# A gated decoder block on one core: the attention branch as seven half-size products, with pooling sums and operand sums on GpSimd

## The chip, the cores and the metric

The kernel runs on one core of a Trainium2 chip. Five engines work beside each other, each with its own queue of instructions: TensorE (PE in the profile, its weight loads PEld), VectorE (DVE), ScalarE (ACT), GpSimd (POOL) and SyncE (SP, which here only issues DMA transfers). The metric is the device time of one execution in microseconds, the median of several.

## The reference

A decoder block on 1024 tokens of 1024 channels, float32. Two mixers run in parallel, a pooling over windows of 2, 4, 8 and 16 tokens and a sliding-window attention; each goes through a branch matrix, is multiplied by its gate, and the sum goes through W_out. An MLP follows.

```python
POOL_WINDOWS = (2, 4, 8, 16)
...
def _multiscale_pool(u, w_pool, pool_scale):
...
        pooled.append((upper - lower) / count)
    pooled = jnp.stack(pooled, axis=2)
    diff = (pooled - uf.reshape(B, S, N_POOL_GROUPS, POOL_GC)).astype(u.dtype)
    mixed = jnp.einsum('bsgc,gcd->bsgd', diff, w_pool)
...
        g = jax.nn.sigmoid(gates.astype(jnp.float32)).astype(x.dtype)
        g_pool, g_attn = g[..., :D_MODEL], g[..., D_MODEL:]
        merged = (g_pool * jnp.einsum('bsc,cd->bsd', y_pool, w_branch_pool[l])
                  + g_attn * jnp.einsum('bsc,cd->bsd', y_attn, w_branch_attn[l]))
        mix = jnp.einsum('bsd,de->bse', merged, w_out[l])
        x = x + _rmsnorm(mix, g_mix_post[l])
```

The attention branch, the part that the change is about, multiplies y_attn (1024 tokens by 512 channels) with w_branch_attn (512 by 1024).

## The kernel before

Activations are kept feature-major: channels on the 128 partitions, the 1024 tokens as two halves of 512 columns. Every float32 operand is split into two parts, a high one that a cast makes (L101, mostly ScalarE) and a low one that a subtraction makes (L104, VectorE), so a product takes three matmul passes: high by high, high by low, low by high.

The stages that matter here follow each other on TensorE: the gates' first products (to about 211 us), the rest of the gates (to 320.5), the attention branch (to 364.0), the pooling branch (to 407.5), W_out, the MLP.

**The gates** (class `Pairs`, L444) are computed as a two-by-two block product with seven half-size products in place of eight. A pair of output rows needs seven weight operands; `operand` (L461) makes sums of weight blocks on VectorE (L467, L470, L474, L477) and splits them (L104). Products 1 and 2 are made in an earlier pass. `rest` (L508) makes 6, 7, 5, 4 and 3 for a pair, twelve matmuls each, and closes each with an addition on VectorE that reads the product out of PSUM (L515, L522, L526, L529, L535), five a pair. Then each gate row is multiplied by the tokens' norm factors (`gate_close1` at L700 over 1024 columns, `gate_close0` at L696 over 512), goes through the sigmoid on ScalarE (L692), and is stored to DRAM by a transfer that ScalarE issues (L693). Eight pairs run through this; a pair is 60 matmuls.

**The attention branch** (`branch`, L908) is a plain product: for each of eight output rows `load_w` (L416) loads and splits a weight tile, and `mm_fm` (L423) makes 24 matmuls, into one PSUM bank for each half of the tokens (L428 and L430). VectorE multiplies the result with the gate (L916). The activations are loaded and split by `load_attn` (L876), called from the last gate pair.

**The pooling sums** (`pool_in`, L668) run on VectorE beside the attention branch: a group's window sum is made by doublings (additions over the whole row, L675, with a short copy for the first columns, L676), then scaled and subtracted (L679 to L681). `pool_part` (L918) loads a group, calls it and splits the result (yphi, yplo) for the pooling branch.

**W_out's operands** are sums of blocks; SP loads one block and GpSimd adds the other by a DMA that accumulates (`wo_add`, L948); a one-column copy by GpSimd (L943) holds the load back until a gate tile is done.

**What sets the order.** In the gates' first pass PE, VectorE, ScalarE and SP stand in an order written out by hand. From `rest` on, a scheduler orders the instructions of each engine, and tile pools decide when a buffer is free. GpSimd serves attention in the early stage, up to 172 us, and then stands idle until 351 us.

Of the kernel before, what the change touches and what calls it, by code (L numbers as in the profile page):

```python
# [14 lines left out]
P = 128  # L15
# [35 lines left out]
def block_kernel(ctx: ExitStack, tc, xt, x, consts, vecs, sinks, b_qkv, g_post, g_mlp_post,  # L51
# [35 lines left out]
    def bank(tag, shape=None):  # L87
        return psum["pool"].tile([P] + (shape or [512]), F32, tag=tag, name=nm(tag), bufs=psum["bufs"][tag])
# [4 lines left out]
    def flat(t):  # L93
        return t.rearrange("p a b -> p (a b)")
# [4 lines left out]
    def split(hi, lo, src, eng=dve, first=None):  # L99
        if first is None:  # L100
            act.copy(hi, src)  # L101
        else:
            first.tensor_copy(hi, src)
        eng.tensor_tensor(lo, src, f32(hi), ALU.subtract)  # L104
# [339 lines left out]
    class Pairs:  # L444


        def __init__(self, src, big, result, close_first, close0, close1):
            self.src, self.big, self.result = src, big, result
            self.close_first, self.close0, self.close1 = close_first, close0, close1
            self.X = {n: [None] * 4 for n in OPERAND.values()}  # L450
            self.raw, self.w, self.sums, self.f0, self.b1 = {}, {}, {}, {}, {}
# [38 lines left out]
        def mm(self, b, p, i, kts=range(4), after=False):  # L490
            w, xo = self.w[p, i], self.X[OPERAND[i]]
            for kt in kts:
                for j, (wh, xh) in enumerate(PASSES):
                    pe.matmul(b, w[:, wh, kt, :], xo[kt][:, xh, :], start=not after and kt == 0 and j == 0,  # L494
                              stop=kt == 3 and j == 2, skip_group_check=after)
# [9 lines left out]
            self.mm(b, p, 2, after=True)  # L505
            self.close_first(self.f0[p][:, :512], b)

        def rest(self, p, f1, b6, b7, b5, done=(), then=None, b4=None):  # L508


            f0 = self.f0.pop(p)
            u2 = f0[:, 512:]
            if 6 not in done:
                self.mm(b6, p, 6)
            dve.tensor_tensor(u2, u2, b6, ALU.add)  # L515
            if p in self.b1:
# [6 lines left out]
            if then:  # L523
                then()
            self.mm(b5, p, 5)
            dve.tensor_tensor(f1[:, 512:], v7, b5, ALU.add)  # L526
            if b4 is None:
                self.mm(b7, p, 4, after=True)
                dve.tensor_tensor(f1[:, :512], u2, b7, ALU.add)  # L529
            else:  # L530
                self.mm(b4, p, 4)
                dve.tensor_tensor(v7, v7, b4, ALU.add)
            self.close1(2 * p + 1, f1)
            self.mm(b5, p, 3, after=True)
            dve.tensor_tensor(u2, u2, b5, ALU.add)  # L535
            self.close0(2 * p, f0)

# [12 lines left out]
    def ar(shape):  # L550
        return ga_.tile([P] + shape, F32R, tag="ga", name=nm("ar"))
# [113 lines left out]
                return  # L665
            owed[0] -= c

    def pool_in(gi, u, place):  # L668

        w = WINDOWS[gi]  # L670
# [9 lines left out]
        dve.tensor_tensor(src[:, :w - 1], src[:, :w - 1], cst[:, C_CNT:C_CNT + w - 1], ALU.mult)  # L680
        dve.tensor_tensor(u[:, :w - 1], src[:, :w - 1], u[:, :w - 1], ALU.subtract)  # L681
        yield

    def y_place():
        return flat(yy.tile([P, 2, 512], F32, tag="y", name=nm("t")))


    def gate_first(f, b):
        dve.tensor_tensor(f, b, rb[:, :512], ALU.mult)
# [13 lines left out]
    def gate_result():  # L703
        return flat(yy.tile([P, 2, 512], F32, tag="y", name=nm("z")))
# [115 lines left out]
    def g32(shape):  # L820
        return gp.tile([P] + shape, F32, tag="g", name=nm("g"))
# [9 lines left out]
    def first(p):  # L831
        gt.m1(p, bank("mm"), g32([S]) if 2 <= p < NHELD else None)
# [10 lines left out]
    with tc.manual_schedule(engines={mybir.EngineType.PE, mybir.EngineType.DVE, mybir.EngineType.Activation,  # L843
# [7 lines left out]
        for p in range(NG0):  # L851
# [19 lines left out]
            elif p == 6:  # L871
                gt.load(2)
                gt.load(3, g32([NK, P]))
    asp = [[None, None], [None, None]]

    def load_attn():  # L876
        for kh in range(2):
            for th in range(2):
                ws = stage([2, 512])
                nc.sync.dma_start(ws, y_dram[th][:, 2 * kh:2 * kh + 2])  # L880
                hi = xp.tile([P, 2, 512], F32R, tag="x", name=nm("yahi"))
                lo = xp.tile([P, 2, 512], F32R, tag="x", name=nm("yalo"))
                split(hi, lo, ws)
                asp[th][kh] = (hi, lo)

    for p in range(8):
        if NHELD <= p + 1 < 8:
            gt.f0[p + 1] = gate_result()
            nc.sync.dma_start(gt.f0[p + 1], z_dram[2 * p + 2])
        if p > 1:  # L890
            gt.load(2 * p)
            gt.load(2 * p + 1, g32([NK, P]) if p > 2 else None)
        for i in (6, 7, 5, 4, 3) if p else (5, 4, 3):
            gt.operand(p, i)
        tag = "at" if p % 2 == 0 else "mm"
        gt.rest(p, gate_result(), bank(tag), bank(tag), bank(tag), then=load_attn if p == 7 else None,
                b4=None if p else bank("mm"))


    zg = {}  # L900

    def gate_pair(base, j):
        zg[base, j] = [g32([2, 512]) for _ in range(2)]
# [4 lines left out]
    def branch(w, rhs, base, m):  # L908
        if m % 2 == 0:
            gate_pair(base, m // 2)  # L910
        z = zg[base, m // 2]
        whi, wlo = load_w(w, [4, P])
        bs = [bank("mm"), bank("mm")]
        mm_fm(bs, whi, wlo, rhs, 4)
        for th in range(2):
            dve.tensor_tensor(z[th][:, m % 2], z[th][:, m % 2], bs[th], ALU.mult)  # L916

    def pool_part(gi):  # L918
        u = yy.tile([P, S], F32, tag="y", name=nm("d"))
        nc.sync.dma_start(u, u_dram[gi])  # L920
        for _ in pool_in(gi, u, y_place):
            pass
        hi = xp.tile([P, S], F32R, tag="x", name=nm("yphi"))
        lo = xp.tile([P, S], F32R, tag="x", name=nm("yplo"))
        split(hi, lo, u)
        ysp[gi] = hi, lo

    gop, wop = {}, {}

    def split_pairs(srcs, place, behind=None):  # L930
        ops = [(place([2, 512]), place([2, 512])) for _ in srcs]
        for hi, _ in ops if behind else ():
            pool.tensor_copy(hi[:, 0, :1], behind[:, 0, :1])
        for (hi, lo), t in zip(ops, srcs):
            split(hi, lo, t)
        return ops

    W_Q = {(a, b): w_o[4 * b:4 * b + 4, :, 512 * a:512 * a + 512] for a in range(2) for b in range(2)}

    def wo_load(quad, place, behind=None):  # L940
        ts = [place([2, 512]) for _ in range(2)]
        for t in ts if behind else ():
            pool.tensor_copy(t[:, 0, :1], behind[:, 0, :1])  # L943
# [11 lines left out]
    def bc32(shape):  # L955
        return bcp.tile([P] + shape, F32, tag="bc", name=nm("s3"))

    ysp = {}
    for m in range(8):
        branch(w_ba[m], lambda k, hl, th: asp[th][k // 2][hl][:, k % 2, :], 8, m)  # L960
        if m == 4:
            sums = wo_load((1, 0), a32, zg[8, 2][1])
            wo_add(sums, (1, 1))
        if m in (2, 3, 5, 6):
            pool_part({2: 1, 3: 0, 5: 2, 6: 3}[m])

    def merge(j):
        for z, zp in zip(zg[8, j], zg.pop((0, j))):
# [1 line left out]

    def merged(kh, th):
        return [zg[8, 2 * kh + j][th] for j in range(2)]

    def x_place(shape):
        return xp.tile([P] + shape, F32R, tag="x", name=nm("wo"))

    b11, b12 = merged(0, 1), merged(0, 0)
    for m in range(8):
# [567 lines left out]
```

## Time and profile before

| | |
|---|---|
| time, median of 3 runs | 1110.98 us (1109.47 to 1111.28) |
| the profiled execution's own time | 1111.93 us |
| its span, first to last instruction | 1110.2 us |
| mean granted TensorE clock | 0.999 |
| ScalarE busy | 549.3 us (49%), 917 instructions |
| DMA | 203.18 MB, mean 183 GB/s |

The page gives busy times by engine, then the chain of work that ended last. A row of the timeline is start, duration, engine, line, operation, output<-input and tile size, all in us; in brackets the idle time before it and what released it. A row of a group ends with its count, busy us and mean ns, and the idle time before. A row of the stretches is a window of the span, with busy us and count of each engine, the granted clock, the DMA share and GB/s.

### The profile page before, as it was taken

The numbers are of one execution on the slowest core, as the hardware profiler recorded it, in microseconds if no ns is written. First come the engines' busy times: TensorE is split into PE (matmuls) and PEld (weight loads), VectorE is DVE, ScalarE is ACT, GpSimd is POOL, SyncE is SP. The second block draws the span as 40 slices with busy tenths as digits, with TensorE's granted clock in tenths as the row PEclk, the third lists the DMA queues.
The fourth block names the chain that finished last, engine by engine and source line by source line (L and its number), as shares of the span: only waits on it lengthen the run. The fifth ranks groups of instructions, "written<-read, shape, count | busy, mean of one in ns | idle before, by whom it ended". The sixth has DMA issues, their size and how long they took to land.

```text
span 1110.2 us, 13876 instructions
## 1 busy us (share of the span) xinstructions
PE 1099.0 (99%) x5119; PEld 908.9 (82%) x5119; DVE 806.3 (73%) x1174; ACT 549.3 (49%) x917; POOL 61.3 (6%) x107
## 2 busy tenths in 40 slices
PE   9999999999999999999999999999999999999997
PEld 7888788888888888878888888888888888888885
DVE  5578867899768796889888767666548944456596
ACT  7466656444432337577555655444434434344342
POOL 0334220000001120000000000000000000000000
PEclk9999999999999999999999999999999999999999
DMA  9405578365677581571457655435596635534672
GB/s 349 140 11 135 150 150 292 122 204 209 212 254 258 150 188 58 193 262 38 151 202 257 237 178 195 155 143 207 172 376 216 204 97 174 178 102 153 201 239 108
DMA packets 88419, 203.18 MB, mean 183 GB/s; under 512 B 7328, under 2 KB 19744, under 8 KB 88352
## 3 DMA queue, kind: packets, MB, share of 16 engines
q1 hardware_dynamic: 76208, 176.35, 47.4%
q10 hardware_dynamic: 5616, 19.66, 4.6%
q0 software_dynamic: 6528, 6.29, 4.1%
q8 instruction: 40, 0.66, 0.2%
q14 instruction: 27, 0.22, 0.1%
HBM read 146.70 MB, written 55.57 MB: 182 GB/s over the span
## 4 chain that ended last, share of the span: by engine, by line
PE 87%; DVE 6%; ACT 2%; DMA 2%; issue 1%; SPq 0%; DVEq 0%; ACTq 0%
PE mm L494 24%; PE at L494 16%; PE at L1390 16%; PE mm L1390 12%; PE mm L428 5%; PE mm L187 3%; PE mm L430 3%; PE mm L584 2%; PE at L196 1%; PE at L1032 1%; PE mm L1032 1%; PE sc L187 1%; PE at L399 1%; PE sc L335 1%; PE mm L196 1%
## 5 line engine op out<-in xcount | busy, mean ns | idle before, releaser
L1390 PE MATMUL at<-ar,wh 128*128 128x512 f32 x744 | 169.6, 389 | 0.0
L1390 PEld LDWEIGHTS at<-ar,wh 128*128 128x128 f32 x744 | 139.6, 188 | 29.3 <-DVE ar L104 0.4
L104 DVE TENSOR_TENSOR wh<-raw,wh 128x1024 fp32r<-128x1024 f32 x53 | 64.8, 1223 | 100.5 <-ACT wh L101 100.4
L1390 PE MATMUL mm<-ar,wh 128*128 128x512 f32 x576 | 131.0, 389 | 0.0
L101 ACT CAST wh<-raw 128x1024 fp32r<-128x1024 f32 x53 | 55.7, 1051 | 147.9 <-PE at L1390 72.1
L1390 PEld LDWEIGHTS mm<-ar,wh 128*128 128x128 f32 x576 | 108.1, 188 | 22.4
L101 ACT CAST wh<-st 128x512 fp32r<-128x512 f32 (+1 forms) x97 | 61.6, 645 | 76.1 <-PE at L494 19.1
L104 DVE TENSOR_TENSOR wh<-st,wh 128x512 fp32r<-128x512 f32 (+1 forms) x97 | 68.8, 719 | 29.4 <-ACT wh L101 27.1
L494 PE MATMUL mm<-gr,wh 128*128 128x512 f32 x333 | 80.4, 391 | 0.6 <-DVE gr L1071 0.6
L494 PEld LDWEIGHTS mm<-gr,wh 128*128 128x128 f32 x333 | 62.1, 188 | 13.7 <-DVE gr L1071 1.0
L494 PE MATMUL mm<-T,wx 128*128 128x512 f32 x288 | 67.6, 389 | 0.0
L494 PEld LDWEIGHTS mm<-T,wx 128*128 128x128 f32 x288 | 54.1, 188 | 11.2
L494 PE MATMUL at<-T,wx 128*128 128x512 f32 x252 | 59.1, 389 | 0.0
L494 PEld LDWEIGHTS at<-T,wx 128*128 128x128 f32 x252 | 47.3, 188 | 9.8
L494 PE MATMUL mm<-x,wh 128*128 128x512 f32 x240 | 55.2, 389 | 0.0
L494 PEld LDWEIGHTS mm<-x,wh 128*128 128x128 f32 x240 | 45.0, 188 | 9.4
L584 PE MATMUL mm<-x,wh 128*128 128x512 f32 x192 | 47.8, 396 | 0.0
L104 DVE TENSOR_TENSOR ar<-B,ar 128x1024 fp32r<-128x1024 f32 x37 | 45.1, 1219 | 3.1 <-ACT ar L101 3.0
L584 PEld LDWEIGHTS mm<-x,wh 128*128 128x128 f32 x192 | 35.2, 188 | 7.7
L101 ACT CAST ar<-B 128x1024 fp32r<-128x1024 f32 x37 | 38.8, 1049 | 4.9 <-DVE B L1365 2.8
L494 PE MATMUL at<-gr,wh 128*128 128x512 f32 x150 | 36.6, 390 | 0.0
L101 ACT CAST wx<-ws 128x512 fp32r<-128x512 f32 x30 | 18.6, 619 | 33.1 <-DVE ws L470 18.2
(387 smaller groups left out, 2162.6 us busy)
## 6 DMA issues: line engine op xcount, KB each, us to landing
raw<-f_dram SPq DMA_DIRECT2D x53, 512.0 KB, 3.7
f_dram<-g SPq DMA_DIRECT2D x30, 512.0 KB, 3.3
B<-in_w_dn_dram SPq DMA_DIRECT2D x24, 512.0 KB, 6.5
st<-in_w_up_dram SPq DMA_DIRECT2D x20, 512.0 KB, 3.8
st<-in_w_g_dram SPq DMA_DIRECT2D x18, 512.0 KB, 4.4
f_dram<-g ACTq DMA_DIRECT2D x17, 512.0 KB, 2.7
g<-spill_dram SPq DMA_DIRECT2D x16, 512.0 KB, 5.6
raw<-in_w_dn_dram SPq DMA_DIRECT2D x16, 512.0 KB, 4.5
```

What stands on the lines that cost most here:

```text
L101: act.copy(hi, src)
L104: eng.tensor_tensor(lo, src, f32(hi), ALU.subtract)
L187: pe.matmul(bq, xs_[k][n // 4][:, xh, n % 4 * P:(n % 4 + 1) * P], wq[k][:, h, :], start=k == 0 and j == 0, stop=k == NK - 1 and j == 2)
L196: pe.matmul(bkv_of(n), xs_[k][n // 4][:, xh, n % 4 * P:(n % 4 + 1) * P], wkv[k // 2][:, h, k % 2, :], start=k == 0 and j == 0 and not (joi ...
L335: pe.matmul(sb[:, kv, i, :nk], qt[r, qx, m * P:(m + 1) * P], kx[r, k0:k0 + nk], start=j == 0, stop=j == 2)
L399: pe.matmul(flat(yb), v[:, kv, :], flat(p[:, 4 * kv:4 * kv + 4]), start=j == 0, stop=j == len(mms) - 1)
L428: pe.matmul(bs[th], whi[:, k, :], rhs(k, hl, th), start=k == 0 and hl == 0, stop=False)
L430: pe.matmul(bs[th], wlo[:, k, :], rhs(k, 0, th), start=False, stop=k == nk - 1)
L494: pe.matmul(b, w[:, wh, kt, :], xo[kt][:, xh, :], start=not after and kt == 0 and j == 0, stop=kt == 3 and j == 2, skip_group_check=after)
L584: pe.matmul(b, (whi, wlo)[h][:, k, :], xr(k, xh, th), start=j == 0, stop=j == len(mms) - 1)
L1032: pe.matmul(bs[t], gop[i][kt // 2][gh][:, kt % 2, t * P:(t + 1) * P], wop[i][kt // 2][wh][:, kt % 2], start=not after and kt == 0 and j == ...
L1390: pe.matmul(bs[t], fo[fh][:, k2, t * P:(t + 1) * P], wo_[wh][:, k2, :], start=not after and s2 == 0 and k2 == 0 and j == 0, stop=s2 == NS ...
```

## The change

Five things change, all between the gates' first pass and W_out.

1. The attention branch becomes a class `Halves`: a two-by-two block product by seven half-size products. Four operands of the activations are taken as they are (B11, B21, B22 and, for T1 to T4, sums made by GpSimd in place by `sums`); three sums of weight blocks a pair are made by GpSimd in `weights` and split there (768 columns), the four plain blocks by VectorE. A pair's products go into two PSUM banks: 1, 2, 6, 7 and 4 add up in one, 5 and 3 in the other; after each step that is needed alone the bank is read out and the next product adds to it.
2. The pooling sums go from VectorE beside the branch to GpSimd beside the gates: `diff_sums` for groups 3, 2, 1 and 0 (windows of 16, 8, 4 and 2), called from pairs 0 to 3, which adds, scales by a table and subtracts, and stores the result back to DRAM by GpSimd's queue. `pool_load` and `pool_split` then only load and split it.
3. `Pairs.rest` calls `side()` after each of its steps, by which the operands of the next pair, the splits of B11 to T3 and GpSimd's work are placed between the products; product 3 is issued ahead of close1.
4. SP and GpSimd stand in program order from the gates' second half to the end of the branch.
5. `wo_load` and `wo_add` for the block (1,0) of W_out stand with pairs 2 and 3 of the branch, without the one-column copies.

```diff
-        def rest(self, p, f1, b6, b7, b5, done=(), then=None, b4=None):
+        def rest(self, p, f1, b6, b7, b5, done=(), side=lambda: None, b4=None):
...
+            side()
+            self.mm(b5, p, 3, after=True)
             self.close1(2 * p + 1, f1)
-            self.mm(b5, p, 3, after=True)
...
+    def diff_sums(gi, place):
+
+        w, u = WINDOWS[gi], diffs.pop(gi)
         act.activation(u, u, AF.Identity, bias=vec[:, V_BU + gi:V_BU + gi + 1])
         src, step = u, 1
         while step < w:
             t = place()
-            dve.tensor_tensor(t[:, step:], src[:, step:], src[:, :S - step], ALU.add)
-            dve.tensor_copy(t[:, :step], src[:, :step])
+            pool.tensor_tensor(t[:, step:], src[:, step:], src[:, :S - step], ALU.add)
+            pool.tensor_copy(t[:, :step], src[:, :step])
             src, step = t, 2 * step
-            yield
-        dve.scalar_tensor_tensor(u[:, w - 1:], src[:, w - 1:], 1.0 / w, u[:, w - 1:], ALU.mult, ALU.subtract)
...
+        cn = cst[:, C_CNT:C_CNT + w]
+        pool.tensor_tensor(src[:, w - 1:], src[:, w - 1:], cn[:, w - 1:].broadcast_to([P, S - w + 1]), ALU.mult)
+        pool.tensor_tensor(src[:, :w - 1], src[:, :w - 1], cn[:, :w - 1], ALU.mult)
+        pool.tensor_tensor(u, src, u, ALU.subtract)
+        pool.dma_start(u_dram[gi], u)
...
+        PRODUCT = {1: ("A11", "B11"), 2: ("A12", "B21"), 3: ("S4", "B22"), 4: ("A22", "T4"),
+                   5: ("S1", "T1"), 6: ("S2", "T2"), 7: ("S3", "T3")}
...
+        def sums(self, part):
+            b11, b12, b21, b22 = (self.raw[q] for q in ((0, 0), (0, 1), (1, 0), (1, 1)))
+            if part == 0:
+                pool.tensor_tensor(b11, b12, b11, ALU.subtract)
+                pool.tensor_tensor(b12, b22, b12, ALU.subtract)
+            else:
+                pool.tensor_tensor(b22, b22, b11, ALU.subtract)
+                pool.tensor_tensor(b21, b21, b22, ALU.subtract)
...
+            pool.tensor_tensor(t[:, 0], a21, a22, ALU.add)
+            pool.tensor_tensor(a21, a11, a21, ALU.subtract)
+            pool.tensor_tensor(t[:, 1], t[:, 0], a11, ALU.subtract)
+            pool.tensor_tensor(t[:, 2], a12, t[:, 1], ALU.subtract)
...
+                split(rh, rl, r.rearrange("p m (h k) n -> p (m h) k n", h=2))
+                split(sh, sl, t[:, :3], pool)
...
+        def mm(self, b, p, i, after=False):
+            wn, xn = self.PRODUCT[i]
+            w, xo = self.wops[p][wn], self.ops[xn]
+            for kt in range(2):
+                for j, (wh, xh) in enumerate(PASSES):
+                    pe.matmul(b, w[wh][:, kt, :], xo[xh][:, kt, :], start=not after and kt == 0 and j == 0,
+                              stop=kt == 1 and j == 2, skip_group_check=after)
...
+            self.mm(y, p, 5)
+            act.copy(t2[:, 0], y)
+            sides[0]()
+            self.mm(x, p, 6, True)
+            act.copy(t[:, 0], x)
+            sides[1]()
+            self.mm(y, p, 3, True)
+            dve.tensor_tensor(t[:, 0], t[:, 0], y, ALU.add)
+            dve.tensor_tensor(z[1][:, 0], z[1][:, 0], t[:, 0], ALU.mult)
+            sides[2]()
+            self.mm(x, p, 7, True)
+            dve.tensor_tensor(t2[:, 0], t2[:, 0], x, ALU.add)
+            dve.tensor_tensor(z[1][:, 1], z[1][:, 1], t2[:, 0], ALU.mult)
+            sides[3]()
+            between()
+            self.mm(x, p, 4, True)
+            dve.tensor_tensor(z[0][:, 1], z[0][:, 1], x, ALU.mult)
...
+    with tc.manual_schedule(engines={mybir.EngineType.SP, mybir.EngineType.Pool}):
+        extra = {(0, 0): lambda: diff_sums(3, xq32), (1, 1): lambda: diff_sums(2, xq32),
+                 (2, 1): lambda: diff_sums(1, xq32), (3, 1): lambda: diff_sums(0, xq32),
+                 (5, 4): lambda: ba.split("B11", x_place), (6, 0): lambda: (ba.sums(0), ba.split("B21", x_place)),
+                 (6, 1): lambda: ba.split("B22", gr),
+                 (6, 2): lambda: ba.sums(1), (4, 2): lambda: w_todo.append(ba.weights(0)),
+                 (7, 0): lambda: (w_todo.pop()(), w_todo.append(ba.weights(1))),
+                 (7, 1): lambda: ba.split("T1", gr), (7, 2): lambda: ba.split("T2", x_place),
+                 (7, 3): lambda: ba.split("T3", x_place)}
```

What stands where on the engines, in program order; a name is a tile with its running numbers. GpSimd before, behind its last store of attention's output (y_dram), where only W_out's pieces (s1) follow:

```order
L404 DMA y_dram<-yt_312_1901 256x1x128 x2
L943 COPY s1_528_3346<-g_522_3309 128x1
L943 COPY s1_529_3347<-g_522_3309 128x1
L950 DMA s1_528_3346<-in_w_o_dram 128x2x512
L950 DMA s1_529_3347<-in_w_o_dram 128x2x512
```

GpSimd with the change at the same place, the first pooling group (q_389 is its row of pooling inputs, q_397 to q_400 the doublings):

```order
L404 DMA y_dram<-yt_312_1901 256x1x128 x2
L682 TENSOR_TENSOR q_397_2375<-q_389_2348 128x1023
L683 COPY q_397_2375<-q_389_2348 128x1
L682 TENSOR_TENSOR q_398_2378<-q_397_2375 128x1022
L683 COPY q_398_2378<-q_397_2375 128x2
L682 TENSOR_TENSOR q_399_2381<-q_398_2378 128x1020
L683 COPY q_399_2381<-q_398_2378 128x4
L682 TENSOR_TENSOR q_400_2384<-q_399_2381 128x1016
L683 COPY q_400_2384<-q_399_2381 128x8
L686 TENSOR_TENSOR q_400_2384<-q_400_2384,cst_82 128x1009
L687 TENSOR_TENSOR q_400_2384<-q_400_2384,cst_82 128x15
L688 TENSOR_TENSOR q_389_2348<-q_400_2384,q_389_2348 128x1024
```

The other three groups follow (10, 8 and 6 rows with their stores), then the weight sums of a pair, the four operand sums and the next pair's weights. VectorE before, in the sixth gate pair (at and mm are PSUM banks, z and g gate rows, ar and wh weight operands, yalo the low part of an activation):

```order
L104 TENSOR_TENSOR yalo_481_3075<-st_479_3072,yahi_480_3074 128x1024
L515 TENSOR_TENSOR g_361_2159<-g_361_2159,mm_448_2837 128x512
L104 TENSOR_TENSOR ar_457_2927<-ws_454_2917,ar_457_2927 128x512
L467 TENSOR_TENSOR ws_466_3016<-g_465_3014 128x512
L522 TENSOR_TENSOR z_447_2836<-g_361_2159,mm_449_2838 128x512
L470 TENSOR_TENSOR ws_466_3016<-ws_466_3016,st_464_3012 128x512
L104 TENSOR_TENSOR yalo_484_3081<-st_482_3078,yahi_483_3080 128x1024
L526 TENSOR_TENSOR z_447_2836<-z_447_2836,mm_450_2839 128x512
```

VectorE with the change at the same place (q_471, q_473 and q_474 are B11, B21 and B22, wo and gr their parts):

```order
L515 TENSOR_TENSOR g_361_2159<-g_361_2159,mm_476_2924 128x512
L104 TENSOR_TENSOR ar_482_2976<-ws_479_2940,ar_482_2976 128x512
L467 TENSOR_TENSOR ws_493_3043<-g_470_2913 128x512
L523 TENSOR_TENSOR z_475_2923<-g_361_2159,mm_477_2925 128x512
L470 TENSOR_TENSOR ws_493_3043<-ws_493_3043,st_469_2911 128x512
L104 TENSOR_TENSOR wo_486_3019<-q_471_2915,wo_485_3018 128x1024
L526 TENSOR_TENSOR z_475_2923<-z_475_2923,mm_478_2926 128x512
L104 TENSOR_TENSOR ar_494_3046<-ws_493_3043,ar_494_3046 128x512
L477 TENSOR_TENSOR st_469_2911<-st_469_2911,g_470_2913 128x512
L104 TENSOR_TENSOR wo_496_3052<-q_473_2919,wo_495_3051 128x1024
```

The closes and the gates' own sums and splits stand as they stood; splits of the activations stand at other places, and four more of them (T1 to T4) come in the last pair. SP with the change, from the load of the first pooling group on (st and g are the gates' weights):

```order
L673 DMA q_389_2348<-spill_dram 128x1024
L458 DMA st_405_2463<-in_w_g_dram 128x1024
L458 DMA g_406_2465<-in_w_g_dram 128x1024
L673 DMA q_407_2467<-spill_dram 128x1024
L458 DMA st_421_2578<-in_w_g_dram 128x1024
L458 DMA st_422_2580<-in_w_g_dram 128x1024
L673 DMA q_423_2582<-spill_dram 128x1024
L458 DMA st_436_2690<-in_w_g_dram 128x1024
L458 DMA g_437_2692<-in_w_g_dram 128x1024
L673 DMA q_438_2694<-spill_dram 128x1024
L458 DMA st_450_2799<-in_w_g_dram 128x1024
L458 DMA g_451_2801<-in_w_g_dram 128x1024
```

Before, only the gates' weights stood there, one behind the other; now the loads of pooling groups, whose buffers GpSimd frees, stand between them.

More of the change, by code (lines that the diff above doesn't have):

```diff
@@ L522, in rest @@
             dve.tensor_tensor(v7, u2, b7, ALU.add)
-            if then:
-                then()
+            side()
             self.mm(b5, p, 5)
             dve.tensor_tensor(f1[:, 512:], v7, b5, ALU.add)
+            side()
             if b4 is None:
@@ L532, in rest @@
                 dve.tensor_tensor(v7, v7, b4, ALU.add)
+            side()
+            self.mm(b5, p, 3, after=True)
             self.close1(2 * p + 1, f1)
-            self.mm(b5, p, 3, after=True)
             dve.tensor_tensor(u2, u2, b5, ALU.add)
             self.close0(2 * p, f0)
+            side()
     wu, wb = {}, {}
@@ L873, in block_kernel @@
                 gt.load(3, g32([NK, P]))
[L874 to L897, printed above, removed]
@@ L902, in gate_pair @@
+    ba = Halves(w_ba, lambda kh, th: y_dram[th][:, 2 * kh:2 * kh + 2], 8)
+    zg, ysp, dif = {}, {}, {}
     def gate_pair(base, j):
@@ L916, in branch, with pool_load, pool_split @@
             dve.tensor_tensor(z[th][:, m % 2], z[th][:, m % 2], bs[th], ALU.mult)
[L918 to L922, printed above, removed]
+    def pool_load(gi):
+        dif[gi] = yy.tile([P, S], F32, tag="y", name=nm("d"))
+        nc.sync.dma_start(dif[gi], u_dram[gi])
+    def pool_split(gi):
         hi = xp.tile([P, S], F32R, tag="x", name=nm("yphi"))
         lo = xp.tile([P, S], F32R, tag="x", name=nm("yplo"))
-        split(hi, lo, u)
+        split(hi, lo, dif.pop(gi))
         ysp[gi] = hi, lo
[L928 to L936, printed above, removed]
     W_Q = {(a, b): w_o[4 * b:4 * b + 4, :, 512 * a:512 * a + 512] for a in range(2) for b in range(2)}
@@ L967, in merge, with split_pairs @@
+    gop, wop = {}, {}
+    def split_pairs(srcs, place, behind=None):
+        ops = [(place([2, 512]), place([2, 512])) for _ in srcs]
+        for hi, _ in ops if behind else ():
+            pool.tensor_copy(hi[:, 0, :1], behind[:, 0, :1])
+        for (hi, lo), t in zip(ops, srcs):
+            split(hi, lo, t)
+        return ops
     def merge(j):
```

131 lines of the change are left out of this document (113 added, 18 removed).

## The prediction

> **What bounds the kernel now.** I read the busy shares first, then the chain of work that ended last, then the stretch that the change touches.
>
> ```profile
> PE 1099.0 (99%) x5119; PEld 908.9 (82%) x5119; DVE 806.3 (73%) x1174; ACT 549.3 (49%) x917; POOL 61.3 (6%) x107
> PE 87%; DVE 6%; ACT 2%; DMA 2%; issue 1%; SPq 0%; DVEq 0%; ACTq 0%
> ```
>
> TensorE (PE) is busy for 99% of a span of 1110.2 us and carries 87% of the chain. A matmul taken away shortens the kernel; work given to another engine costs time only where TensorE comes to wait for it. So the question is the slack of the other engines where the new work is put. That is the second half of the gates; I cut it by TensorE's own steps, one gate pair to a row, from 225 us to the branch at 320.5.
>
> ```profile
> core 0: us, PE busy (x) PEld busy (x) DVE busy (x) ACT busy (x) POOL busy (x), PEclk, DMA share, GB/s
> 225.00:238.80 13.80, 13.80 (x63) 11.42 (x62) 12.95 (x21) 6.26 (x9) 0.00 (x0) 1.00 0.55 172
> 238.80:252.50 13.70, 13.70 (x62) 11.36 (x61) 13.24 (x22) 6.54 (x10) 0.00 (x0) 1.00 0.64 217
> 252.50:266.10 13.60, 13.60 (x62) 11.26 (x61) 12.88 (x21) 6.10 (x10) 0.00 (x0) 1.00 0.65 223
> 266.10:279.70 13.60, 13.60 (x62) 11.26 (x61) 11.73 (x17) 7.30 (x10) 0.00 (x0) 1.00 0.56 198
> 279.70:293.20 13.50, 13.50 (x62) 11.16 (x61) 10.75 (x15) 6.54 (x8) 0.00 (x0) 1.00 0.74 230
> 293.20:306.90 13.70, 13.70 (x62) 11.17 (x61) 9.62 (x14) 4.51 (x6) 0.00 (x0) 1.00 0.69 233
> 306.90:320.50 13.60, 13.60 (x62) 11.26 (x61) 7.12 (x10) 4.08 (x5) 0.00 (x0) 1.00 0.74 251
> ```
>
> TensorE never waits here, GpSimd (POOL) does nothing, ScalarE (ACT) is half idle. VectorE (DVE) is the tight one: 78.3 us of 95.5, summed over the rows, which leaves it 17.2 us, and little of that in the first three pairs. How far it runs ahead of TensorE shows in one operand of pair 1:
>
> ```profile
> 232.23 0.69 DVE L104 TENSOR_TENSOR wh<-st,wh 128x512 fp32r<-128x512 f32 x1
> 236.04 1.52 PE L494 MATMUL mm<-x,wh 128*128 128x512 f32 x6
> ```
>
> The split ends at 232.92, its product starts at 236.04: a lead of 3.1 us. A VectorE that loses more than the lead and its idle time stops TensorE.
>
> **What is removed.** The attention branch lies between these rows:
>
> ```profile
> 320.48 0.39 PE L428 MATMUL mm<-yahi,wh 128*128 128x512 f32 x1
> 364.00 0.39 PE L428 MATMUL mm<-yphi,wh 128*128 128x512 f32 x1
> ```
>
> That is 43.52 us for 192 matmuls, 0.2267 us each. Seven products of 2 x 3 matmuls for each of four pairs make 168, so 24 go: **5.44 us**, if nothing stalls. The two accumulator chains of a pair make each product wait for the reader of the one before; the new order on TensorE puts other products between them, so I cost that at nothing; if that cover fails, the price is at most one eviction of 0.69 us (the row of L526 below) for each of 16 steps, 11 us; the shortest filler is four matmuls, 0.9 us, so I stay at nothing.
>
> VectorE's pooling sums leave the branch, where TensorE did not wait for them: 0 gained. The pieces of W_out that GpSimd adds by DMA lose the one-column copies that held them back; TensorE uses them after the pooling branch: 0 too.
>
> **What is added to VectorE.** It splits seven operands of 1024 columns and two weight tiles of 1024 beside the gates, where it had four such splits, two small weight splits and one pooling sum.
>
> ```profile
> 286.41 1.22 DVE L104 TENSOR_TENSOR yalo<-st,yahi 128x1024 fp32r<-128x1024 f32 x1
> 260.41 0.69 DVE L104 TENSOR_TENSOR ar<-ws,ar 128x512 fp32r<-128x512 f32 x1
> 261.01 0.68 DVE L526 TENSOR_TENSOR z<-z,mm 128x512 f32<-128x512 f32 x1
> 261.61 0.68 DVE L104 TENSOR_TENSOR ar<-st,ar 128x512 fp32r<-128x512 f32 x1
> ```
>
> Back to back such an operation costs 0.60 us at 512 columns (from start to start above) and, by the same overlap of 0.08, 1.14 at 1024: 5 x 1.14 - 1.14 - 2 x 0.60 = **3.4 us** more. Alone, that fits into the 17.2.
>
> **What is added to GpSimd.** From the order: 18 additions or products of 1009 to 1024 columns and 14 short ones for the pooling sums, then four operand sums of 1024, and for two weight pairs eight sums of 256 and two splits of 768. The trace has only shorter ones:
>
> ```profile
> L104 POOL TENSOR_TENSOR v<-vf,v 128x128 fp32r<-128x128 f32 x8 | 3.7, 462 | 0.4
> L275 POOL TENSOR_TENSOR qkv<-qkv,cst 128x160 f32<-128x160 f32 x5 | 2.6, 528 | 25.3 <-DVE qkv L268 25.3
> L277 POOL TENSOR_TENSOR qkv<-qkv,rb 128x80 f32<-128x80 f32 x5 | 1.8, 355 | 0.1
> L404 POOL DMA_DIRECT2D y_dram<-yt x16 | 16.5, 1174 | 38.3 <-ACT s L101 15.3 <-DMA y_dram<-yt 11.2 <-ACT wh L101 9.0
> ```
>
> From 80 to 160 columns 173 ns more, 2.2 ns a column; carried on, 1024 columns take about 2.43 us, 768 about 1.85, 256 about 0.74; each of the four stores that GpSimd now issues is 1.17. That is 53.5 us for the 22 long ones, 5.9 for the sums of 256, 3.7 for the splits, 4.7 for the stores, some 69 with the short ones, beside 95 us in which GpSimd was idle. By busy time alone it fits. (The Trainium skill, "GPSIMD Engine Reference", section "3. Performance versus the Vector engine", gives 4497 ns for 2048 columns; by it a long one would be 2.25 us, an estimate, and the holds worked out next 4 us less in sum. No run so far shows that width.)
>
> **What they cost each other.** The trace shows the two side by side at a few places only. In the attention stage:
>
> ```profile
> 58.00 0.52 POOL L276 TENSOR_TENSOR rb<-y,cst 128x160 f32<-128x160 f32 x1
> 58.10 0.45 DVE L353 TENSOR_TENSOR es<-snk,nmx 128x8 f32<-128x8 f32 x1
> L353 DVE TENSOR_TENSOR es<-snk,nmx 128x8 f32<-128x8 f32 x7 | 1.2, 168 | 0.2
> ```
>
> An operation of eight columns with two inputs in SBUF takes 0.168 us elsewhere (mean of seven) and 0.45 when it meets a GpSimd operation that started first: it ends 0.03 us after it. The other way round:
>
> ```profile
> 392.93 1.22 DVE L104 TENSOR_TENSOR gr<-g,gr 128x1024 fp32r<-128x1024 f32 x1
> 394.06 0.68 DVE L104 TENSOR_TENSOR wh<-st,wh 128x512 fp32r<-128x512 f32 x1
> 394.66 1.22 DVE L993 TENSOR_TENSOR g<-g,g 128x1024 f32<-128x1024 f32 x1
> 393.08 2.97 POOL L943 COPY s<-g 128x1 f32<-128x1 f32 x2 [4.76 <-DVE g L916]
> ```
>
> Two GpSimd copies of one column take 2.97 us: they sit behind three VectorE operations without a gap, which end at 395.88. But where VectorE reads PSUM, both run at their own length:
>
> ```profile
> 55.77 0.47 POOL L104 TENSOR_TENSOR v<-vf,v 128x128 fp32r<-128x128 f32 x1
> 55.81 0.69 DVE L104 TENSOR_TENSOR qt<-at,qt 128x512 fp32r<-128x512 f32 x1 [0.54 <-ACT qt L101]
> ```
>
> So the two exclude each other for a whole operation when VectorE has both inputs in SBUF, and who starts first keeps the other out. The Trainium skill ("SBUF — State Buffer", section "🔬 SBUF: two separate sides") has this as a rule: the shared port pair is an exclusive lock, held for the instruction, against a VectorE operation with two SBUF inputs. The rows above agree in both directions; none shows it for GpSimd operations of over 160 columns. With that rule the sum below stands, without it the 5.44 us are all that is left.
>
> In the gates a GpSimd operation can start when VectorE reads PSUM (five closes a pair) or idles. If it starts with a close, the next VectorE operation is free 0.60 us later and is held until 0.14 us before GpSimd's end (the held one above ended at 58.55 and needs 0.168, so it was let go at 58.38, and GpSimd's ended at 58.52): 2.43 - 0.60 - 0.14 = 1.69 us for a long one, 1.85 - 0.74 = 1.1 for a split of 768, nothing for a sum of 256. The 14 short operations lie between nothing and the 0.35 us of an operation of 80 columns; nearest is nothing, since a close covers them, so I take 1 us for all. The unknown is whether a long one holds VectorE for its whole length: the bounds are 0 and 1.69 us, and I take 1.69, as each of the rows shows a full hold.
>
> 22 x 1.69 + 2 x 1.1 + 1 = 40.4 us of holds, and 3.4 of more work, against 17.2 idle and a lead of 3.1: **23.5 us** of waiting for TensorE. Some holds will come after the gates, since GpSimd gets only some five starts a pair and has 46 operations; there VectorE has slack. If the four operand sums' holds (6.8 us) move there, 16.7 remain. I take **20**.
>
> So the profiled execution of 1111.93 us becomes 1111.93 - 5.44 + 20 = 1126.5. The median of the runs is 0.95 us under the profiled execution: **1125.5**.
>
> **What is queued behind GpSimd.** GpSimd's and SyncE's (SP) queues now stand in program order. The load of the third pooling group waits for a buffer that the third copy of the first group frees, that of the fourth for the first group's store; the gates' weights for pairs 5 and 6 stand behind these on SP. ScalarE's three later bias operations stand ahead of casts of pairs 2 to 5. While GpSimd is less than about a pair late, weights asked for two pairs ahead cover that.
>
> **Rivals.**
>
> **A, no hold at these lengths (0.20).** VectorE does its own 3.4 us in its slack; 1111.93 - 5.44 - 0.95 = 1105.5. For it: VectorE and GpSimd have time enough by busy sums. Against it: every overlapping row above.
>
> **B, the holds stop TensorE (0.59), the forecast and the slower side.** Place: the gates, 225 to 320. It decides as soon as the holds pass 17.2 + 3.1 - 3.4 = 16.9 us, and the kernel is slower than before once they pass 16.9 + 5.44 = 22.3, or 1.0 us for each of the 22. Own range: 16.7 - 5.44 over the median before, 1122, to 23.5 with the short ones at their 0.35 us (4 us more), 1133; a tenth off the carried-on 2.43 us is 22 x 0.24 = 5 us either way, half of which I add: 1119 to 1136.
>
> **C, holds shared with idle time (0.14).** If half of the long operations start where VectorE waits for a close anyway, 20 us of holds are left: 20 + 3.4 - 20.3 = 3 us of waiting, 1108.6; with two thirds some 10 us, 1115. Range 1107 to 1118.
>
> **D, GpSimd starved (0.07).** If VectorE, behind its plan, leaves no gaps, the first group's 12 operations take 12/5 pairs, the buffers come late, and the weights of a pair stand still on SP. One pair late is 13.6 us more than B: 1139.
>
> **How the numbers follow.** A measurement of this kernel can tell about 0.2%, that is 2.2 us, from no change. Faster: A and a seventh of C, 0.22. Same (1108.8 to 1113.2): a third of C, 0.05. Slower: 0.73. The range goes from A's 1105.5, less the 1.5 us by which single runs fall under the median, to B's end: 1104 to 1136, with D's half above it left out. B's own range is 1119 to 1136.
>
> **What would show each step.** The branch's 168 matmuls in 38.1 us without waits: the first term. VectorE's two-input operations in the gates with lengths of 2 to 2.5 us instead of 0.68, each ending just after a GpSimd operation, and TensorE waits released by VectorE's splits: B. The same lengths as before and pairs of 13.6 us: A. GpSimd operations of much over 2.4 us, waits of TensorE on DMA or ScalarE: D. I am wrong by size if a long GpSimd operation is not near 2.4 us, and wrong in kind if VectorE's operations keep their lengths beside it.

## The result, and the profile after

With the change the kernel takes **1138.87 us** (median of 6 runs, 1137.33 to 1139.45) against 1110.6 before: a ratio of 1.0254, 95% interval 1.0241 to 1.0267. It is slower, as forecast, and by 2.9 us more than the range allowed. The busy shares and the chain of the profile after:

```profile
span 1136.9 us, 13919 instructions
PE 1104.7 (97%) x5095; PEld 909.5 (80%) x5095; DVE 841.1 (74%) x1153; ACT 561.6 (49%) x932; POOL 148.1 (13%) x165
PE 64%; DVE 4%; issue 1%; ACT 1%; DMA 0%; DVEq 0%; ACTq 0%
```

TensorE has 24 matmuls fewer and is busy for longer: 1104.7 us against 1099.0. So there are two losses, time in which it waits and matmuls that take longer. By stage (windows of the span; columns as in the profile before, cut at the gates up to product 4 of pair 4, the rest of the gates, the branch without its last six matmuls, the pooling branch):

```profile
225.00:300.39 75.39, 59.81 (x229) 46.38 (x228) 74.72 (x69) 28.44 (x37) 55.17 (x40) 0.86 0.50 176
300.39:351.78 51.39, 46.47 (x194) 37.88 (x193) 43.32 (x45) 23.20 (x26) 25.47 (x16) 0.93 0.64 222
351.78:390.00 38.22, 37.12 (x163) 30.07 (x162) 31.21 (x39) 18.09 (x24) 10.24 (x7) 1.00 0.76 235
390.00:434.00 44.00, 44.00 (x196) 36.27 (x195) 35.23 (x43) 12.59 (x15) 9.52 (x8) 1.00 0.73 207
```

In the first stage VectorE is busy for 74.72 of 75.39 us with 69 instructions, 1.08 us each, where before a row of one pair had 21 in 12.9, 0.62 each. TensorE is busy for 59.81 and its granted clock is 0.86. The last two stages run at full clock. What VectorE's time went into, GpSimd's rows and VectorE's of the same five microseconds:

```profile
231.61 2.35 POOL L682 TENSOR_TENSOR q<-q 128x1020 f32<-128x1020 f32 x1
233.91 0.65 POOL L683 COPY q<-q 128x4 f32<-128x4 f32 x1
234.63 2.36 POOL L682 TENSOR_TENSOR q<-q 128x1016 f32<-128x1016 f32 x1
```

```profile
231.52 0.69 DVE L470 TENSOR_TENSOR ws<-ws,st 128x512 f32<-128x512 f32 x1
232.25 2.26 DVE L477 TENSOR_TENSOR st<-st,st 128x512 f32<-128x512 f32 x1
234.43 0.68 DVE L523 TENSOR_TENSOR z<-z,mm 128x512 f32<-128x512 f32 x1
235.03 2.52 DVE L474 TENSOR_TENSOR st<-st,ws 128x512 f32<-128x512 f32 x1
```

L477 and L474 are sums of weights that took 0.68 or 0.69 us before; now each ends when a GpSimd addition has ended and its own 0.6 us have passed. L523 reads PSUM and keeps its 0.68. GpSimd's additions are held too: one that meets only a VectorE operation reading PSUM takes 1.89 us.

```profile
226.15 1.89 POOL L682 TENSOR_TENSOR q<-q 128x1023 f32<-128x1023 f32 x1 [54.02 <-ACT q L678]
```

Between 224 and 288 us exactly 18 of VectorE's 54 operations are longer than their like before, as many as GpSimd has long ones there, by 29.3 us in sum or 1.63 us each; up to 345 us it is 40.1 us. The view of TensorE's waits shows what came of it (its longest rows for the gates and the branch):

```profile
PE mm L494 <- DVE z L523: 8.7, 2, 6.8
PE at L494 <- DVE z L523: 6.6, 2, 4.9
PE at L494 <- ACT wh L101: 4.6, 1, 4.6
PE at L946 <- DVE g L977: 1.1, 1, 1.1
```

TensorE waits for a close: product 4 adds to the bank that L523 must have read, and L523 stands on VectorE behind held operations (the cast waits for a weight sum behind such a hold). What follows a wait:

```profile
231.00 2.20 PE L494 MATMUL mm<-gr,ar 128*128 128x512 f32 x9
235.16 0.97 PE L494 MATMUL mm<-T,wh 128*128 128x512 f32 x3 [1.96 <-DVE z L523]
235.97 3.44 PE L494 MATMUL mm<-gr,wh 128*128 128x512 f32 x9
239.21 3.41 PE L494 MATMUL mm<-x,wh 128*128 128x512 f32 x12
242.45 0.84 PE L494 MATMUL at<-T,ar 128*128 128x512 f32 x3
```

```profile
236.00:237.00 1.00, 1.00 (x5) 0.85 (x4) 1.00 (x1) 0.25 (x1) 1.00 (x2) 0.83 0.00 0
238.00:239.00 1.00, 1.00 (x4) 0.81 (x3) 1.00 (x2) 0.19 (x1) 1.00 (x1) 0.50 0.00 0
239.00:240.00 1.00, 1.00 (x3) 0.44 (x2) 1.00 (x2) 0.00 (x0) 1.00 (x2) 0.50 0.00 0
241.00:242.00 1.00, 1.00 (x7) 0.79 (x6) 1.00 (x1) 0.00 (x0) 1.00 (x1) 1.00 0.89 172
```

Nine matmuls take 2.20 us before the wait and 3.44 behind it, and 1.8 us are lost on top of the wait. The granted clock is 0.50 in four stretches of the gates (columns as above):

```profile
236.66:240.07 3.41, 3.41 (x10) 2.35 (x8) 3.41 (x4) 0.62 (x1) 3.39 (x4) 0.50 0.00 0
253.72:260.55 6.83, 5.14 (x12) 3.80 (x12) 6.83 (x6) 2.29 (x3) 6.67 (x7) 0.50 0.18 72
274.20:284.44 10.24, 5.49 (x12) 3.80 (x12) 10.24 (x12) 4.33 (x6) 6.70 (x7) 0.50 0.63 202
328.82:335.64 6.82, 5.69 (x13) 4.46 (x14) 5.21 (x6) 1.78 (x2) 5.11 (x5) 0.50 0.24 77
```

They last one, two, three and two times 3.41 us, and they start 5, 6 and 16 times 3.41 us apart.

From matmul start to matmul start over the whole stretch, each distance less the 0.2267 us of a matmul at full clock, starts more than 0.6 us apart add 23.3 us of waiting, and starts 0.24 to 0.6 us apart add 10.2 us of slow matmuls. 23.3 + 10.2 - 5.44 = 28.1; W_out starts at 435.04 in place of 407.52, 27.5 us later.

### The profile page after: what moved, and what is told of

Same layout as the page of the kernel before. It is cut to its first block, busy times and chain, and to the rows that moved or that the text cites. A ratio compares the mean times of both kernels' runs of the same rounds, so it can differ in the third digit from the quotient of the medians.

```text
span 1136.9 us, 13919 instructions
## 1 busy us (share of the span) xinstructions
PE 1104.7 (97%) x5095; PEld 909.5 (80%) x5095; DVE 841.1 (74%) x1153; ACT 561.6 (49%) x932; POOL 148.1 (13%) x165
## 4 chain that ended last, share of the span: by engine, by line
PE 64%; DVE 4%; issue 1%; ACT 1%; DMA 0%; DVEq 0%; ACTq 0%
PE mm L494 16%; PE at L1542 15%; PE at L494 12%; PE mm L1542 11%; PE mm L428 3%; PE mm L946 2%; PE at L946 1%; PE mm L430 1%; PE at L1184 1%; PE mm L1184 1%; DVE x L1199 1%; DMA st<-in_w_up_dram 0%; DVE st L1200 0%; PE at L1230 0%; DVE wh L104 0%
## 5 line engine op out<-in xcount | busy, mean ns | idle before, releaser
L104 DVE TENSOR_TENSOR wh<-st,wh 128x512 fp32r<-128x512 f32 (+1 forms) x94 | 75.6, 815 | 26.8 <-ACT wh L101 24.3
L101 ACT CAST wh<-st 128x512 fp32r<-128x512 f32 (+1 forms) x94 | 61.4, 664 | 67.9 <-PE at L494 14.7
L494 PE MATMUL mm<-gr,wh 128*128 128x512 f32 x333 | 83.5, 402 | 0.2 <-DVE gr L1223 0.2
L494 PE MATMUL at<-T,wh 128*128 128x512 f32 x138 | 36.4, 405 | 11.3 <-DVE z L523 6.6
L494 PEld LDWEIGHTS at<-T,wh 128*128 128x128 f32 x138 | 26.2, 193 | 18.0 <-DVE z L523 7.5
```

## The experiments

Each run stands beside runs of the kernel before on the same chip (medians of 1109.45 to 1110.82 us). "Waiting" and "slow matmuls" are worked out from the trace as above.

**GpSimd writes only.** In the change's pooling sums:

```diff
-            pool.tensor_tensor(t[:, step:], src[:, step:], src[:, :S - step], ALU.add)
-            pool.tensor_copy(t[:, :step], src[:, :step])
+            for _ in range(2):
+                pool.memset(t[:, step:], 0.0)
+            pool.memset(t[:, :step], 0.0)
```

The scaling and the subtraction become writes of zeros in the same way.

> The pooling sums are left out: GpSimd's 18 long and 14 short pooling operations, which read SBUF, become writes of zeros to the same tiles (two for each long one), in the same order and with the same stores. Theory 1 (a GpSimd operation that reads SBUF holds VectorE's operations with two SBUF inputs): VectorE's operations between 225 and 290 us keep 0.68 and 1.22 us, TensorE's waits there (2.0, 4.6, 6.8, 0.4 and 1.7 us) and the halved clock behind them go; what is left are the operand sums' holds near 312 to 330, one wait of about 5 us with some 3 us of halved clock; 1111 to 1117 us. Rival (the new order of VectorE, SP and GpSimd makes the closes late, whatever GpSimd does): 1133 to 1140 us, waits at the same places.

1114.7 us (one run). Two rows of GpSimd and three of VectorE at the place shown above:

```profile
229.23 1.99 POOL L683 MEMSET q<- 128x1023 f32 x2
233.13 1.96 POOL L683 MEMSET q<- 128x1020 f32 x2
```

```profile
229.96 0.69 DVE L477 TENSOR_TENSOR st<-st,st 128x512 f32<-128x512 f32 x1
231.23 0.69 DVE L474 TENSOR_TENSOR st<-st,ws 128x512 f32<-128x512 f32 x1
233.95 0.68 DVE L104 TENSOR_TENSOR wh<-st,wh 128x512 fp32r<-128x512 f32 x1
```

GpSimd is as long at work with a pair of writes (1.97 us) as with an addition that has its way (1.89), on the same queue with the same stores, and no VectorE operation is held beside a write. The three that are longer before 288 us (1.10 to 1.28 us, from 267 to 272 us) stand beside GpSimd's weight sums, which read SBUF. All waits before 300 us are gone; left are those of the operand sums (4.9 us and 2.2 of slow matmuls in one place). The rival, the new order, falls.

**The same sums on VectorE, at the same places.** In `diff_sums` the engine is VectorE, with the fused scaling and subtraction of the kernel before:

```diff
-            pool.tensor_tensor(t[:, step:], src[:, step:], src[:, :S - step], ALU.add)
-            pool.tensor_copy(t[:, :step], src[:, :step])
+            dve.tensor_tensor(t[:, step:], src[:, step:], src[:, :S - step], ALU.add)
+            dve.tensor_copy(t[:, :step], src[:, :step])
```

> The pooling sums go to VectorE at the same places of the program, 14 long operations in place of GpSimd's 18, stored as before by GpSimd's queue. Theory 1: 14 x 1.14 = 16 us of VectorE's own work in place of 29 us of holds, against some 20 us of slack shared with 3.4 us of other new work and 10 us of holds by the operand and weight sums: waits of 5 to 12 us in sum, 1112 to 1124 us, that is faster than with GpSimd. Rival (VectorE is short of time, GpSimd relieves it): VectorE gets 16 us more to do than in the change, so slower than 1138.9 us, 1145 to 1155.

1127.26 us, ratio 1.0153 [1.0138, 1.0168]: 3 us over theory 1, and 11.6 faster than with GpSimd's help. VectorE is better off doing the work itself than being relieved of it. Waiting 18.1, slow matmuls 5.9; the operand and weight sums still hold it for 14.7 us.

**The sums spread out.** Windows 16 and 8 in gate pairs 2 and 3, windows 4 and 2 beside the branch, all on VectorE:

```diff
-        extra = {(0, 0): lambda: diff_sums(3, xq32), (1, 1): lambda: diff_sums(2, xq32),
-                 (2, 1): lambda: diff_sums(1, xq32), (3, 1): lambda: diff_sums(0, xq32),
+        extra = {(2, 1): lambda: diff_sums(3, xq32), (3, 1): lambda: diff_sums(2, xq32),
...
+    def pool_sums(gi):
+        if gi < 2:
+            diffs[gi] = dif[gi]
+            diff_sums(gi, lambda: flat(yy.tile([P, 2, 512], F32, tag="y", name=nm("t"))), False)
```

> The pooling sums on VectorE, the two wide windows in gate pairs 2 and 3, the two narrow ones beside the branch, loaded there as they are; the products in halves and GpSimd's operand and weight sums stay. Theory 1: 10 us of the sums in the gates, 6 us in the branch where VectorE has room; with the operand sums' holds the gates are just full: waits of 0 to 6 us, 1105 to 1112 us. Rival (the branch in halves has waits of its own in its two chains): at least 4 us of waits inside the branch, over 1110 us.

1120.67 us, ratio 1.0096 [1.0079, 1.0112]. Both theories miss: there is no wait before 300 us and 1.3 us in the branch; 10.7 us of waiting lie between 300 and 328 us. GpSimd's operand and weight sums hold VectorE for 15.2 us from 285 to 334 us, which I had taken for 10.

**Pauses without GpSimd.** In the kernel before, `delay` additions ahead of the close of product 7 (0, 5, 6, 7, 8, 9, 11, 13 by pair):

```diff
+            for _ in range(delay):
+                dve.tensor_tensor(v7, u2, u2, ALU.add)
             dve.tensor_tensor(v7, u2, b7, ALU.add)
```

> The kernel before, with 5, 6, 7, 8, 9, 11 and 13 additions of 512 columns put in VectorE's queue ahead of one close in gate pairs 1 to 7, so that TensorE pauses for growing lengths with GpSimd idle; the result is unchanged. Theory 1 with a halved clock behind a pause: pauses of about 1 to 6 us; behind those of over 2.2 us the next 16 to 26 matmuls come 0.43 us apart in place of 0.2267, 2 to 3 us lost for each; short pauses lose nothing. Rival (the halved clock belongs to the overlap with GpSimd, or to the products, not to the pause): all matmuls behind the pauses stay at 0.2267 us.

1129.96 us (one run). The scheduler moved products into some pauses; five of over 1 us were left. One of 2.2 us, with GpSimd idle for the whole stage, shows the same picture, nine matmuls in 3.60 us:

```profile
318.72 0.96 PE L494 MATMUL at<-T,wh 128*128 128x512 f32 x3 [2.06 <-DVE z L524]
319.52 3.60 PE L494 MATMUL at<-gr,wh 128*128 128x512 f32 x9
```

A later one of 7.6 us lost 1.8; those of 1.1, 1.8 and 2.5 us lost 0.1 to 0.2. So the halved clock belongs to pauses, not to GpSimd; but the pause of 2.5 us, which theory 1 had losing 2 to 3 us, kept the full clock. To find the length, 8, 9, 10 and 10 additions in pairs 1, 3, 5 and 7 alone:

> The kernel before with 8, 9, 10 and 10 additions of 512 columns ahead of one close in gate pairs 1, 3, 5 and 7, none in the others, to get four pauses of 2 to 3.5 us with GpSimd idle. If the length of the pause decides, those over some length between 1.9 and 3.2 us all cost 1.4 to 2.8 us of halved clock and those under it nothing; if where the pause falls decides, two pauses of nearly the same length differ (the change had 2.1 us with 1.8 us lost and the sums on VectorE 2.4 us with 0.2 us lost).

1118.79 us (one run). The scheduler filled all but two pauses over 1 us, 1.6 us (0.1 lost) and 3.5 us (1.7 lost), so this run by itself does not tell length from place.

**The products alone.** No pooling sums at all, operand and weight sums on VectorE (`dve` for `pool` in `sums` and `weights`):

> The pooling sums (and the bias ahead of them) are left out: the groups are loaded and split as they are; operand sums and weight sums go to VectorE, so GpSimd only issues DMA. Theory 1: the 24 matmuls taken away are worth their 5.44 us once nothing holds VectorE: 1104 to 1107 us, no wait of TensorE over 1 us in the gates. Rival (the two accumulator chains of the branch cost something of their own): waits inside the branch of 2 to 10 us, 1107 to 1115 us.

1106.39 us, ratio 0.9962 [0.9949, 0.9975]: 4.2 us faster than before. No wait in the gates; two small ones in the branch (1.8 us in sum) cover the rest of the 5.44, which lies inside the interval (2.8 to 5.7 us). The same with these sums on GpSimd:

> The same without the pooling sums, but operand sums and weight sums on GpSimd as in the change. Theory 1: their holds (about 14 us in the version with split pooling sums) now meet a VectorE with 17 us of slack less 3.4 us: waits of 0 to 6 us with up to 3 us of halved clock, 1105 to 1113 us, slower than with these sums on VectorE. Rival (the pooling sums alone are to blame): the same time as with these sums on VectorE, within 1 us.

1115.12 us, ratio 1.0033 [1.0019, 1.0048], 8.7 slower for moving eight operations of 256 and two of 768 columns in the gates, four of 1024, and as many weight sums in the branch, off VectorE. One wait of 5.5 us and 2.1 of slow matmuls behind it are most of it. Pooling sums are not the only ones to blame.

**All sums on VectorE**, with one wide window in the gates, then with two:

> All sums on VectorE: the widest window's pooling sums in gate pair 2, the three others beside the branch, operand and weight sums in place of GpSimd's. Theory 1: in the gates 5.7 us of pooling sums, 9 of operand and weight sums and 3.4 of splits fill 18 of 20 us; the branch gets 10 us of pooling sums and is full: waits of 0 to 6 us, 1105 to 1111 us. Rival (VectorE has no room left for 19 us more in 177): 1111 to 1118 us.

> As the version before, but the two wide windows' sums in gate pairs 2 and 3 and the two narrow ones beside the branch. Theory 1: in the gates 23 us against 20, so some waits: 3 to 8 us with a halved clock, 1108 to 1115 us; faster than the same version with GpSimd's operand and weight sums (1120.7 us) by the difference of holds (15 us) and own work (9 us), 4 to 10 us. Rival (GpSimd relieves VectorE there): slower than 1120.7 us.

1114.78 [ratio 1.0023 to 1.005] and 1115.62 us [1.0032 to 1.0062]. Without any holds VectorE is still full, in the first from 280 to 364 us without a gap over 0.7 us: waits of 7.1 us with 3.3 of slow matmuls in the one, of 8.4 with 1.2 in the other. The first theory falls to its rival; the second run is 0.6 us over its theory's range, and 5 us better than with GpSimd's sums, as that theory had it.

**Less work for VectorE.** In these two, windows 8 and 16 become one running sum each, and window 2 one subtraction, halved by ScalarE:

```diff
+            dve.tensor_tensor_scan(t[:, :w], u[:, :w], u[:, :w], 0.0, ALU.add, ALU.bypass)
+            dve.tensor_tensor_scan(t[:, w:], u[:, w:], u[:, :S - w], t[:, w - 1:w], ALU.add, ALU.subtract)
```

> As the version with all sums on VectorE and one wide window in the gates (1114.8 us), but the two wide windows' sums as one running sum each (a scan that adds the new column and subtracts the one that leaves the window) in place of three and four doublings, and window 2 as one subtraction, halved by ScalarE. Theory 1 (VectorE's time is the bound): if the scan takes 2.2 us for 1024 columns (it has no row in any trace here; an ordinary operation of that width is 1.22, so 1.1 to 2.4), VectorE has 4.6 us less to do, and waits with their halved clock shrink from 10 us to 3 to 6: 1107 to 1111 us. Rival (the waits come from where the sums stand, not how long they are): 1113 to 1116 us.

> The same in the version with two wide windows in the gates (1115.6 us). Theory 1: 4.6 us less for VectorE, 3.5 of them in the gates: 1108 to 1112 us. Rival (place, not length): 1114 to 1117 us.

The scan's row, and that of the one subtraction:

```profile
L693 DVE TENSOR_TENSOR_SCAN q<-q,q 128x1016 f32<-128x1016 f32 x1 | 2.3, 2329 | 0.0
L681 DVE TENSOR_TENSOR t<-d 128x1023 f32<-128x1023 f32 x1 | 1.2, 1227 | 0.0
```

A scan costs two ordinary operations and stands for three or four. 1108.07 us, ratio 0.9989 [0.998, 0.9998], and **1105.43 us, ratio 0.9957 [0.994, 0.9973]**: faster than both kernels, the second 2.6 us under the range of its theory 1. In the second TensorE waits once in the gates, for 0.8 us, and its clock is not halved before its last matmul. That is 10 us for 4.5 us of VectorE's work: the waits go, and the slow matmuls with them.

**Where that gain comes from.** The kernel before with only its pooling sums made so:

> The kernel before with only its pooling sums made as in the faster version (running sums for windows 8 and 16, one subtraction for window 2), the branch as a plain product. Theory 1 (before, VectorE had slack beside the branch, so its time there is worth nothing; the gain of the faster version is that of the products in halves): 1109 to 1111 us, no change. Rival (the shorter pooling sums are themselves the gain): 1104 to 1107 us.

1110.02 us, ratio 0.9995 [0.9985, 1.0004]: no change. The shorter sums are worth nothing where VectorE has slack; they make room for the products.

## Why the prediction was wrong

**The matmuls (5.44 us): right.** The products alone gave 4.2 of them, with 5.44 inside the interval. The chains, which I costed at nothing, take at most the rest; what shows of them there is one wait of 1.2 us for ScalarE's copy out of a bank (L970) and one of 0.2. The first is longer than the 0.69 us that I had as the most for a step.

**VectorE's own 3.4 us: right.** They fit into its slack; with the products alone the gates have no wait.

**The holds (40.4 us): right in sum, and that by luck.** 40.1 us were measured. A long GpSimd operation takes 1.89 us, not the carried-on 2.43 and not the 2.25 of the other estimate; but it does not start beside a close, with 0.60 us for free, as I had it. In the rows above one VectorE operation passes between two of GpSimd's, turn for turn, and the next is held for nearly the whole of it: 1.63 us where I had 1.69. Two errors of over half a microsecond each cancel. That GpSimd gets only five starts a pair was wrong too; it did all its pooling sums by 287 us. The rule of the Trainium skill ("SBUF — State Buffer", section "🔬 SBUF: two separate sides") holds at 1024 columns as well, and its limit to GpSimd operations that read SBUF is what the writes show: 0.69 us beside them.

**The waiting (20 us, 23.5 by the full sum): right.** 23.3 us. The step from 23.5 down to 20 was not borne out: GpSimd kept pace, and the four operand sums ran before the branch, by 329 us. I named the splits as releasers; it was mostly the closes behind them, L523 for 15.3 of some 21 us in the view of waits.

**What failed is the sum "1111.93 - 5.44 + 20": it prices a wait of TensorE at its length.** It has no term for the matmuls behind the wait. With four of the change's pauses the clock is halved, for 3.41 to 10.24 us, and the matmuls behind them lost 1.8 to 2.8 us each, 10.2 us in all with the small change of others. With the 23.3 us of waiting alone the kernel would have come to about 1128, inside the range; with the clock it is 1139, outside. (That is addition; no run has the waits without the slow matmuls, and a slower TensorE also gives VectorE time to catch up.)

In the trace before TensorE never paused for as long as a microsecond between two matmuls. The halved clock shows there only at the two ends, where I did not look:

```profile
1.53 4.30 PE L205 MATMUL mm<-zeros 128*128 128x512 f32 x11 [1.53 <-DVE zeros L183]
1107.30:1110.00 2.70, 0.00 (x0) 0.00 (x0) 0.00 (x0) 0.00 (x0) 0.00 (x0) 0.50 0.38 140
```

Of the first eleven matmuls those from 2.12 to 4.68 us start 0.43 us apart, the last ones 0.23; and 4.3 us behind the last matmul of all the granted clock falls to 0.50. The Trainium skill could have told more: "TensorE: Matmul & The Clock Gate", section "What's actually happening", has the array at half clock after an idle window of about 3.4 us, in a window that runs free of the work, until a busy one has passed. The traces agree on the 3.41 us and on the free run, and differ in one point: the window need not be idle for its whole length.

Over all runs here the 13 pauses of 3.2 to 7.6 us all lost 0.9 to 2.8 us; of five between 2.0 and 2.5 us two lost 1.7 and 1.8, three 0.2 at most; no shorter one lost over 0.4 by itself. Length alone does not sort them, the place does. In each run the halved stretches begin and end on one grid of 3.41 us. Laid on it, the clock fell 15 times in all the traces before the last matmul, each time behind an interval of the grid in which TensorE had idled for 1.92 us or more; behind the intervals with 1.88 us or less it never fell. The two pauses of 2.1 and 2.2 us that were paid for lay with 1.92 and 2.10 us in one interval; the three of 2.0 to 2.5 us that cost nothing were spread over two. This was read from the traces afterwards; no run was made to test it.

**The rivals.** A and C fall with the holds. D's late buffers did not show: no wait of TensorE for DMA in the gates, and its one long wait for ScalarE goes back to a held weight sum. That D's 1139 us is the time measured is chance.

## What to carry to other kernels

A free engine is no free time: before work goes to GpSimd beside a busy VectorE, count each long GpSimd operation that reads SBUF as VectorE's own time (1.63 us each here, more than the 1.14 us that VectorE needs for such an addition itself), since here it was better to leave the sums on VectorE and best to make them shorter. Where TensorE is the bound, price a pause of over two to three microseconds at its length and about two more for the slow matmuls behind it; here the slow matmuls added nearly half as much again to the waits. Here a pause under 1.9 us cost by itself hardly more than its length. And a saving on the bound engine needs room on the engines that feed it: with all the pooling sums in, a gain of 4 to 5 us came out only when VectorE's work shrank by as much.

## What the runs showed of the hardware that was not expected

GpSimd's addition of two rows of 1023 columns takes 1.89 us, where carrying on from 80 and 160 columns had given 2.43. A one-column copy by GpSimd takes 0.65 us beside a busy VectorE; a write of one column takes 0.10, so most of the copy is likely its turn of waiting. In the rows at 231 to 237 us the two engines take turns, one operation each, while both have work queued. GpSimd's write of 1024 columns takes 0.96 us, and no VectorE operation beside one was longer than its like. In the gates and the branch TensorE's clock was halved for whole multiples of 3.41 us, on a grid that the work did not set, and 1.92 us of idling inside one interval of it were enough. A scan on VectorE takes 2.33 us for 1016 columns, against 1.22 us for an ordinary two-input operation of that width.
